# Cross-attention's planned order: the load queue chained into it, and key scaling planned no earlier than the block's start

## The chip, the cores and the metric

The kernel runs on one core of one Trainium2 chip. The metric is the time of one execution on the device in microseconds (us): the median over several runs, beside it the span and the instructions of one execution that was profiled.

## The reference

A two-layer encoder over 512 tokens of width 1024, all in float32. Each layer is a mixer, then memory cross-attention, then a gated convolutional FFN, each with a residual sum. Layer 0 mixes with forgetting and differential attention, layer 1 with a chunkwise mLSTM. The change lies in cross-attention (4 heads of 256, 256 memory tokens), which runs once per layer:

```python
def memory_cross_attention(xn, memn, wq, wkv, wo):
    q = split_heads(xn @ wq, XATTN_HEADS)
    k, v = jnp.split(memn @ wkv, 2, axis=-1)
    k = split_heads(k, XATTN_HEADS)
    v = split_heads(v, XATTN_HEADS)
    logits = jnp.einsum('bhqd,bhmd->bhqm', q, k, preferred_element_type=jnp.float32) * (XATTN_HEAD_DIM ** -0.5)
    p = jax.nn.softmax(logits, axis=-1)
    out = jnp.einsum('bhqm,bhmd->bhqd', p.astype(v.dtype), v)
    return merge_heads(out) @ wo
...
    for layer in range(DEPTH):
        ...
        x = x + mixed
        x = x + memory_cross_attention(rms_norm(x, xattn_norm[layer]), rms_norm(mem, mem_norm[layer]),
                                       xattn_wq[layer], xattn_wkv[layer], xattn_wo[layer])
```

## The kernel before, in words

**Products in three parts.** Every float32 operand is split into a high and a low part, and a product is three matmuls (high x high, high x low, low x high). The activations are held transposed, in eight tiles `x0` to `x7` of 128 x 512, with `xh`/`xl` beside them. A weight comes in chunks of 128 x 1024: SP loads it into one of three `raw` buffers, ScalarE (ACT) casts it to `wh`, and VectorE (DVE) subtracts to get `wl`, after which the raw buffer is free. `wh` and `wl` also have three buffers each, which the planner counts as `h` slots; such a slot is free when the chunk's matmuls are done.

**Cross-attention's stages on TensorE (PE).** (1) Two value blocks, the opening: V of 512 columns each, four chunks per block (c0 to c7 over both), two steps of six matmuls of 512 columns per chunk, into two accumulator banks per block (lines 1375 to 1377). In between come the eight small matmuls of the norm of x (line 1256). (2) The query projection: head 0 plainly (`plain`), heads 1 to 3 with seven instead of eight products of halves (`seven`), with the blocks of K and head 0's scores in between. (3) Scores, transposes, weighted values. (4) The output projection, eight blocks.

**What comes from the stage before.** The mixer's output projection is eight blocks of 5.2 us on PE; after each, DVE adds to `x` and the next stage's `xh`, `xl` and squares are made. Before it, two K products for the keys ("fills", each with two of the eight key blocks) were already made; they sit in two of the four accumulator banks until `keys` has scaled them. `keys(m)` multiplies the product by the memory's norm (DVE, into `kx`, one buffer), ACT casts it to `kt` and DVE subtracts the low part. The second `kx` of a pair frees the bank. The tiles of cross-attention's own pool (`kx`, `kt`, `sa`, `q` and others) lie in space which the mixer's pool held before; the pools for `raw`, `wh`, `wl` and `x` are shared by all stages.

**Other transfers of the stage.** `leave` stores each `x` tile to memory (`xs<-x`, line 1304), since the tiles are then used as room by the sevens; `back` loads it again before the output projection (`x<-xs`, line 1311). The planner lets `leave` follow `form`, which makes the sums of x that the sevens need. A seven loads one weight half into `sa` (two buffers), and POOL's queue adds another onto it by an accumulating transfer. All plain loads of this stage are issued at line 1193.

**What sets the order.** `Sched` is a planner that runs while the kernel is built. Each task has an engine, a duration, dependencies, a due time worked back from the matmul that needs it, and the buffers that it takes and frees; time 0 is the start of the opening on PE, and SP may begin 14 us and ACT and DVE 10.4 us ahead of it. It picks tasks engine by engine and calls each task's function, which emits the instructions. `after` is a lower limit on a task's planned time, and a buffer's slot holds the planned time from which it is free (line 1174 sets the three of `h`). The tile framework then schedules what was emitted on every engine by its own rules. For the engines in `ORDERED`, `planned(True)` ties each instruction to the one emitted before it on the same engine, so that the framework keeps the planner's order there. In the kernel before, these are DVE, ACT and POOL; PE and SP are not tied. The FFN's planner calls `planned` in the same way. On the chip each engine runs its instructions in order, and each waits for what its data need.

Of the kernel before, what the change touches and what calls it, by code (L numbers as in the profile page):

```python
# [62 lines left out]
def restored(ps):  # L63

    return ps.rearrange("p (k r) -> p r k", r=2)


def folded(ap):

    return ap.rearrange("p (r k) -> p r k", r=2)  # L70


ORDERED = ("vector", "scalar", "gpsimd")


class Item:
    def __init__(self, fn, dur, deps, prio, take, free, chain, pre, after, order, load, st):
        self.fn, self.dur, self.deps, self.prio, self.st = fn, dur, list(deps), prio, st
        self.take, self.free, self.chain, self.pre, self.after = take, free, chain, pre, after
        self.order, self.load = [o for o in order if o is not None], load  # L80
        self.ready = None
# [4 lines left out]
class Plan:  # L86
# [11 lines left out]
    def add(self, fn, dur=0.0, deps=(), prio=None, take=(), free=(), chain=(), pre=(), after=0.0, order=(), load=(), st=None, soon=False):  # L98
        it = Item(fn, dur, [d for d in deps if d is not None], len(self.items) if prio is None else prio, take, free, chain, pre, after, order, load, st)
        it.n, it.soon = len(self.items), soon  # L100
        self.items.append(it)
        return it
# [215 lines left out]
class Engines:  # L318
# [6 lines left out]
    def __getattr__(self, name):  # L325
        return getattr(self.nc, name)

    def planned(self, on):
        for c in self.chains:
            c.on, c.last = on, None  # L330


class Builder:
    def __init__(self, tc, t):
        self.tc, self.nc, self.t = tc, Engines(tc, ORDERED), t
        self.uid = 0
# [831 lines left out]
    def xattn_steps(self, layer, mp):  # L1168

        nc, t = self.nc, self.t  # L1170
        sc = Sched(
            WAIT, raw=3, h=3, sa=2, sb=2, ra=1, s2=1, a22=1, s4=1, qc=1, v=1, u2=1, u3=1, kx=1, q=6, kt=3, e=7, pt=2, acc=4, s=2, w=2
        )
        sc.slots.update(h=[-10.4, -5.2, 0.0])
        add = sc.add
        tt = lambda n: 0.055 + 1.06e-3 * n
        act = lambda n: 0.1 + 0.83e-3 * n
        tt_ = nc.vector.tensor_tensor
        clock = [0.0]
# [136 lines left out]
        def keys(m, get, deps, free=()):  # L1316
            st = {}

            def scaled():
                if m % 2 == 0:  # L1320
                    kt[m // 2] = self.til(mp, "kt", (P, 2, 2, MEM), F32R, bufs=3)
                st["x"] = self.til(mp, "kx", (P, MEM), bufs=1)
                tt_(out=folded(st["x"][:]), in0=restored(get()), in1=folded(self.memrb[:]), op=ALU.mult)

            take = [("kx", st)] + ([("kt", kst[m // 2])] if m % 2 == 0 else [])
            a = add("DVE", tt(256), scaled, deps, clock[0] + 0.5, take, free)
            h = add("ACT", act(256), lambda: nc.scalar.copy(kt[m // 2][:, 0, m % 2, :], st["x"][:]), [a], clock[0] + 1.0)
            kdone[m // 2].append(
                add("DVE", tt(256), lambda: self.sub(kt[m // 2][:, 1, m % 2, :], st["x"][:], kt[m // 2][:, 0, m % 2, :]), [h], clock[0] + 1.5, (), [("kx", st)])
            )  # L1330
# [3 lines left out]
        def key_block(m):  # L1334
            st, lo = weight(t["xk"][layer, m], clock[0])
            xh, xl = self.mems()
            last = None
            for c in range(2):

                def fn(c=c):  # L1340
                    if c == 0:
                        st["ps"] = self.acc_bank(st["_acc"])
                    for k in range(4 * c, 4 * c + 4):
                        s = slice(k * P, (k + 1) * P)
                        self.mm3(st["ps"][:, :MEM], st["wh"][:, s], st["wl"][:, s], xh[k], xl[k], k == 0, k == 7)

                last = pe(1.335, fn, [lo, last], [("acc", st)] if c == 0 else (), [("h", st)] if c else ())
                if c == 0:
                    yield
            keys(m, lambda: st["ps"][:, :MEM], [last], [("acc", st)])  # L1350
# [275 lines left out]
        for b, st in enumerate(self.fills):  # L1626
            st["_acc"] = st["banks"][0]
            sc.slots["acc"][st["_acc"]] = float("inf")
            sc.held.append(st)
            for i in range(2):  # L1630
                keys(2 * b + i, lambda st=st, i=i: st["ps"][:, i * MEM : i * MEM + MEM], (), [("acc", st)] if i else ())
# [19 lines left out]
        for k in range(4):  # L1651
            f, a, st = form(k, FORM + 4.0 * k)
# [36 lines left out]
        for m in range(8):  # L1689
            for _ in out_block(m):  # L1690
                pass
        nc.planned(True)
        sc.run()
        nc.planned(False)
        self.state = state


# [770 lines left out]
```

## Time and profile before

| | |
|---|---|
| median of 3 runs | 1422.31 us (1421.45 to 1422.38) |
| the profiled execution | 1424.06 us, of which the span is 1422.30 us |
| PE busy, matmuls | 1399.5 us, 98% of the span |
| DVE busy | 1169.5 us, 82% |
| ACT busy | 859.9 us, 60% |
| transfers | 204.75 MB, 144 GB/s in the mean |
| granted PE clock | 0.999 |
| openings of cross-attention | 254.45 to 281.96 us (layer 0), 940.61 to 968.12 us (layer 1) |

A time between two executions can differ by some tenths of a percent, and the span leaves out what lies around the first and last instruction. In rows of the profile, `L306` is the line through which nearly all instructions of DVE, ACT and POOL are emitted, so those are told apart by their tiles (`out<-in`); SP's rows are the issue of a transfer, not its duration.

### The profile page before, as it was taken

To read this page: it belongs to the slowest core of one execution; us is meant where nothing else is said; L and a number is where in the kernel's file an instruction comes from. 1 tells how busy PE (TensorE), PEld (TensorE's weight loads), DVE (VectorE), ACT (ScalarE), POOL (GpSimd) and SP (SyncE) were. 2 spreads that over 40 slices of the span, in tenths; PEclk is the share of its full clock that TensorE was granted. 3 is DMA by queue.
4 is the path that set the end of the run, shared out by engine and by line. 5 is a ranking of instruction groups with operands and counts; after the bars stand their busy time and mean duration, and the time that the engine had idled before them with its cause. 6 is when DMAs were issued, how large, how long until landed. Compare 5 with 4: busy or idle time off the path is not lost.

```text
span 1422.3 us, 22959 instructions
## 1 busy us (share of the span) xinstructions
PE 1399.5 (98%) x8660; PEld 1263.0 (89%) x8660; DVE 1169.5 (82%) x2006; ACT 859.9 (60%) x1444; POOL 138.4 (10%) x201
## 2 busy tenths in 40 slices
PE   9999999899999999999999999999999999999998
PEld 8888868799889999999888888979988999999997
DVE  7787786788689999999768876668877999999984
ACT  6797565666475656666456665456655665656655
POOL 0002220010001111110001121001000111111000
PEclk9999999999999999999999999999999999999999
DMA  5225325663258776774233332466413877777622
GB/s 205 90 58 152 111 81 180 212 161 116 90 156 222 185 182 175 188 178 118 73 116 103 128 98 80 159 190 185 149 60 122 212 198 176 191 177 187 142 75 80
DMA packets 77183, 204.75 MB, mean 144 GB/s; under 512 B 8352, under 2 KB 8352, under 8 KB 77072
## 3 DMA queue, kind: packets, MB, share of 16 engines
q1 hardware_dynamic: 61888, 163.44, 35.5%
q0 software_dynamic: 14176, 38.72, 15.8%
q8 instruction: 68, 1.11, 0.3%
q10 hardware_dynamic: 1008, 1.12, 0.2%
q14 instruction: 43, 0.35, 0.1%
HBM read 196.91 MB, written 6.34 MB: 143 GB/s over the span
## 4 chain that ended last, share of the span: by engine, by line
PE 83%; DVE 9%; ACT 3%; issue 2%; DMA 2%; POOL 0%; POOLq 0%; DVEq 0%; ACTq 0%
PE acc L384 17%; PE acc L385 17%; PE acc L386 17%; PE w L384 4%; PE w L386 4%; PE w L385 4%; PE s L384 3%; PE s L386 3%; PE s L385 3%; DVE wl L306 2%; PE acc L446 1%; PE acc L448 1%; PE acc L447 1%; DMA raw<-in_xv_dram 1%; PE w L2244 1%
## 5 line engine op out<-in xcount | busy, mean ns | idle before, releaser
L306 ACT CAST wh<-raw 128x1024 fp32r<-128x1024 f32 (+2 forms) x223 | 228.2, 1025 | 179.2 <-PE acc L385 90.5
L306 DVE TENSOR_TENSOR wl<-raw,wh 128x1024 fp32r<-128x1024 f32 (+2 forms) x223 | 267.0, 1198 | 40.0 <-ACT wh L306 39.3
L384 PE MATMUL acc<-xh,wh 128*128 128x512 f32 (+1 forms) x752 | 251.7, 335 | 0.0
L386 PE MATMUL acc<-xh,wl 128*128 128x512 f32 (+1 forms) x752 | 250.1, 333 | 0.0
L385 PE MATMUL acc<-xl,wh 128*128 128x512 f32 (+1 forms) x752 | 250.1, 333 | 0.0
L386 PEld LDWEIGHTS acc<-xh,wl 128*128 128x128 f32 x752 | 143.1, 190 | 11.1
L384 PEld LDWEIGHTS acc<-xh,wh 128*128 128x128 f32 x752 | 143.3, 191 | 10.2
L385 PEld LDWEIGHTS acc<-xl,wh 128*128 128x128 f32 x752 | 143.2, 190 | 10.2
L306 DVE SCALAR_TENSOR_TENSOR c<-hs,vec,c 128x512 f32<-128x512 f32 x176 | 131.8, 749 | 3.8 <-ACT c L306 0.8
L384 PE MATMUL w<-ah,wh 128*128 128x512 f32 x304 | 115.7, 381 | 0.2 <-ACT c L306 0.2
L385 PE MATMUL w<-al,wh 128*128 128x512 f32 x304 | 115.2, 379 | 0.0
L386 PE MATMUL w<-ah,wl 128*128 128x512 f32 x304 | 115.2, 379 | 0.0
L306 DVE TENSOR_TENSOR x<-acc,x 128x512 f32<-128x512 f32 (+1 forms) x43 | 28.0, 654 | 67.8 <-PE acc L386 67.8
L306 ACT CAST ah<-c 128x512 fp32r<-128x512 f32 x44 | 27.2, 619 | 85.5 <-DVE c L306 85.5
L306 ACT ACTIVATE c<-hs,vec 128x512 f32<-128x512 f32 x88 | 70.8, 812 | 13.1 <-DVE hs L306 8.8
L386 PEld LDWEIGHTS w<-ah,wl 128*128 128x128 f32 x304 | 57.5, 189 | 8.1
L384 PEld LDWEIGHTS w<-ah,wh 128*128 128x128 f32 x304 | 57.6, 190 | 7.9 <-DVE x L306 0.9
L385 PEld LDWEIGHTS w<-al,wh 128*128 128x128 f32 x304 | 57.6, 190 | 6.5
L386 PE MATMUL acc<-mem,wl 128*128 128x256 f32 (+1 forms) x192 | 59.6, 310 | 1.1 <-DVE wl L306 1.1
L384 PE MATMUL acc<-mem,wh 128*128 128x256 f32 (+1 forms) x192 | 59.6, 310 | 0.1
L385 PE MATMUL acc<-mem,wh 128*128 128x256 f32 (+1 forms) x192 | 59.5, 310 | 0.0
L306 POOL DMA_DIRECT2D sa<-in_up_dram x36 | 31.6, 877 | 279.0 <-DVE hs L306 114.3
(443 smaller groups left out, 4041.0 us busy)
## 6 DMA issues: line engine op xcount, KB each, us to landing
raw<-in_up_dram SPq DMA_DIRECT2D x52, 512.0 KB, 4.0
sa<-in_up_dram SPq DMA_DIRECT2D x36, 512.0 KB, 3.5
sa<-in_up_dram POOLq DMA_DIRECT2D x36, 512.0 KB, 6.7
raw<-in_down_dram SPq DMA_DIRECT2D x32, 512.0 KB, 4.1
ra<-in_up_dram SPq DMA_DIRECT2D x36, 256.0 KB, 4.4
sb<-in_up_dram POOLq DMA_DIRECT2D x36, 256.0 KB, 5.0
raw<-in_wo_dram SPq DMA_DIRECT2D x16, 512.0 KB, 4.0
raw<-in_xk_dram SPq DMA_DIRECT2D x16, 512.0 KB, 3.7
```

What stands on the lines that cost most here:

```text
L306: i = issue(*a, **k)
L384: mm(out, wh, xh, start=first, stop=False, skip_group_check=parts)
L385: mm(out, wh, xl, start=False, stop=False, skip_group_check=parts)
L386: mm(out, wl, xh, start=False, stop=last, skip_group_check=parts)
L446: mm(ps, xh[k][:, ts], wh, start=(k == 0), stop=False)
L447: mm(ps, xh[k][:, ts], wl, start=False, stop=False)
L448: mm(ps, xl[k][:, ts], wh, start=False, stop=(k == 7))
L2244: nc.tensor.matmul(ps[:, lo:], vv[s][:, c], a[:], start=(s == 0), stop=(s == 3))
```

## The change

Three edits, all in how cross-attention is planned:

- SP is wrapped like the other ordered engines, and cross-attention ties all four in the planner's order. `planned` takes how many engines it ties, three unless told otherwise, so the FFN's order is tied as before.
- The slots of `sa` are free in the plan from 1.0 on, instead of from -14.
- The first operation of `keys`, the multiplication into `kx`, is planned at 0.3 at the earliest. Without a limit it could be planned from -10.4 on, when DVE's plan begins.

No instruction is added or removed.

```diff
-ORDERED = ("vector", "scalar", "gpsimd")
+ORDERED = ("vector", "scalar", "gpsimd", "sync")
...
-    def planned(self, on):
-        for c in self.chains:
+    def planned(self, on, n=3):
+        for c in self.chains[:n]:
             c.on, c.last = on, None
...
-        sc.slots.update(h=[-10.4, -5.2, 0.0])
+        sc.slots.update(h=[-10.4, -5.2, 0.0], sa=[1.0, 1.0])
...
-            a = add("DVE", tt(256), scaled, deps, clock[0] + 0.5, take, free)
+            a = add("DVE", tt(256), scaled, deps, clock[0] + 0.5, take, free, after=0.3)
...
-        nc.planned(True)
+        nc.planned(True, 4)
         sc.run()
-        nc.planned(False)
+        nc.planned(False, 4)
```

## The prediction

> **What bounds the kernel now.** I read the busy shares first, then the matmul engine's waits over the whole span, then a table of windows, and last the timelines of PE, DVE, ACT and SP around one of those waits. Busy time and waits come first:
>
> ```profile
> PE 1399.5 (98%) x8660; PEld 1263.0 (89%) x8660; DVE 1169.5 (82%) x2006; ACT 859.9 (60%) x1444; POOL 138.4 (10%) x201
> PE acc L1376 <- DVE wl L306: 5.5, 8, 1.0
> PE acc L1375 <- ACT wh L306: 1.6, 2, 1.0
> ```
>
> PE is busy for 1399.5 of 1422.3 us, so only its gaps can be won. The two longest rows of its waits (us in total, times, longest) belong to L1375 and L1376, matmuls of the value blocks with which cross-attention opens. The windows of layer 0's opening and of the stretch behind it show it (columns: window, length, busy us of PE, its loads, DVE, ACT, POOL, granted clock, DMA share, GB/s):
>
> ```profile
> 254.40:282.00 27.60, 23.31 (x106) 18.77 (x106) 22.76 (x36) 19.81 (x28) 1.78 (x2) 1.00 0.79 237
> 282.00:300.00 18.00, 18.00 (x118) 16.71 (x117) 16.58 (x25) 10.93 (x17) 5.13 (x4) 1.00 0.69 188
> ```
>
> PE is full behind the opening and has holes inside it. Now the PE timeline there (start, duration, tile, and in brackets the idle time before it with what ended it):
>
> ```profile
> 254.45 0.38 PE L1375 MATMUL acc<-wh,mem 128*128 128x512 f32 x1
> 255.40 0.48 PE L1375 MATMUL acc<-wh,mem 128*128 128x512 f32 x1 [0.57 <-DVE x L306]
> 256.86 0.48 PE L1376 MATMUL acc<-wl,mem 128*128 128x512 f32 x1 [0.98 <-DVE wl L306]
> 259.56 0.95 PE L1256 MATMUL s<-ones,sq 128*128 128x2 f32 x8
> 260.37 0.46 PE L1376 MATMUL acc<-wl,mem 128*128 128x512 f32 x1
> 263.82 0.38 PE L1377 MATMUL acc<-wh,mem 128*128 128x512 f32 x1
> ...
> 268.13 0.38 PE L1377 MATMUL acc<-wh,mem 128*128 128x512 f32 x1
> 269.55 0.48 PE L1375 MATMUL acc<-wh,mem 128*128 128x512 f32 x1 [1.04 <-ACT wh L306]
> 270.81 0.48 PE L1376 MATMUL acc<-wl,mem 128*128 128x512 f32 x1 [0.78 <-DVE wl L306]
> 279.48 0.48 PE L1376 MATMUL acc<-wl,mem 128*128 128x512 f32 x1 [0.64 <-DVE wl L306]
> 281.96 0.38 PE L384 MATMUL acc<-xh,wh 128*128 128x512 f32 x1
> ...
> 940.61 0.38 PE L1375 MATMUL acc<-wh,mem 128*128 128x512 f32 x1
> 968.12 0.38 PE L384 MATMUL acc<-xh,wh 128*128 128x512 f32 x1
> ```
>
> The pace of full matmuls is 0.216 us (20 of them from 263.82 to 268.13). The opening holds 16 steps of 6 such matmuls, 96 x 0.216 = 20.7 us, and the eight small ones of L1256, 0.8 us (259.56 to 260.37): 21.5 us. It lasts from 254.45 to 281.96, and in layer 1 from 940.61 to 968.12: 27.5 us each. So each opening loses 6.0 us, 11.9 us both together before rounding, more than the brackets add up to since a matmul after a wait is also 0.1 us slower.
>
> **Why it waits.** The eight chunks of the value weights (c0 to c7) go through three raw buffers: load (SP), `wh` (ACT), `wl` (DVE), which frees the buffer. Here are these engines:
>
> ```profile
> 244.12 1.05 ACT L306 CAST wh<-raw 128x1024 fp32r<-128x1024 f32 x1 [2.99 <-issue]
> 249.47 0.69 DVE L306 TENSOR_TENSOR x<-acc,x 128x512 f32<-128x512 f32 x1 [2.29 <-PE acc L386]
> 252.06 1.46 SPq L1193 DMA_DIRECT2D sa<-in_xq_dram  x2
> 254.65 0.69 DVE L306 TENSOR_TENSOR x<-acc,x 128x512 f32<-128x512 f32 x1 [2.34 <-PE acc L386]
> 255.26 0.41 DVE L306 TENSOR_TENSOR kx<-acc,memrb 128x256 f32<-128x256 f32 x1
> 255.59 1.22 DVE L306 TENSOR_TENSOR wl<-raw,wh 128x1024 fp32r<-128x1024 f32 x1
> 256.53 0.39 ACT L306 CAST kt<-kx 128x256 fp32r<-128x256 f32 x1
> 256.82 1.04 ACT L306 CAST wh<-raw 128x1024 fp32r<-128x1024 f32 x1
> 256.87 0.34 SPq L1193 DMA_DIRECT2D raw<-in_xv_dram  x1
> 258.78 1.22 DVE L306 TENSOR_TENSOR wl<-raw,wh 128x1024 fp32r<-128x1024 f32 x1
> 260.03 8.33 DMA raw<-in_xv_dram
> 265.37 0.42 DVE L306 TENSOR_TENSOR kx<-acc,memrb 128x256 f32<-128x256 f32 x1
> 272.01 1.22 DVE L306 TENSOR_TENSOR wl<-raw,wh 128x1024 fp32r<-128x1024 f32 x1
> 285.28 0.69 DVE L306 TENSOR_TENSOR x<-sa,raw 128x512 f32<-128x512 f32 x1
> ```
>
> c0's `wh` is done at 245.2, yet its `wl` runs at 255.59, though DVE stood idle for over 2 us twice in between. What stands ahead of it on DVE is the key scaling `kx`, at 255.26, directly behind the last `x` of the output projection. The plan allows `kx` at once and DVE is held to the plan's order, but on the chip `kx` comes only with the end of the projection. I infer that its space belongs to the stage before until then; the trace doesn't name that wait. ACT does the same one step on: c1's `wh` (256.82) stands behind `kt` (256.53). So the buffers are freed late: c3's load goes at 256.87, when c0's `wl` ends, c4's at 260.03, when c1's ends, and c4's load, 8.33 us on the chain of waits, makes the holes at 269.55 and 270.81.
>
> **The change, part by part.**
>
> *Keys not before 0.3.* `kx` and all behind it on its chain leave the front of the order; no instruction is added. c0's `wl` can then follow its `wh`, at about 245.2. c1's `wh` needs an h slot, free when the projection's seventh block ends (its `x` is at 249.47), so its `wl` is at about 250.4 to 251.6, in idle time of DVE. It pushes that block's later vector work by about 1 us; no matmul waits for that. c3's load then goes at 246.4 and c4's at 251.7, 10.5 and 8.3 us sooner. From there, with t = 0 at 254.45 and chunks of 12 x 0.216 = 2.59 us:
>
> - First matmuls: c0 is ready; the second accumulator bank still waits for `x` (254.65 + 0.69), so the wait that 255.40 ends is the next limit. 0.65 us of matmuls fit before it: 0.3 us, 0.4 with the slow matmul. This remains.
> - c3 and c4 are in memory before their h slots are free: nothing.
> - c2, c3 and c4 get their h slots at the ends of the projection, of c0 and of c1: t = 0, 3.0 and 6.4 (with the hole above and 0.8 of small matmuls). 1.05 of ACT and 1.22 of DVE later their raw buffers are free, and the loads of c5, c6 and c7 go at about 2.5, 5.4 and 8.7. With the slow 8.33 us landing and again ACT and DVE they are ready at 13.1, 16.0 and 19.3; PE wants them at 14.2, 16.8 and 19.4, so they just fit. The first query weight behind them (load at 13.1) would be ready at 23.7 against 22.0: 1.7 us late, or, with the median landing of 4.7 us (below), early. I take 0.5.
> - DVE: 22.76 us busy of 27.60 now; two `wl` leave it (2.4), so 20.3 stand against 22.8. It is nearly full, and the last hole (279.48, 0.64 idle, 0.8 with the slow start) was its lateness. I keep half, 0.4.
>
> *The load queue in the plan's order, `sa` from 1.0.* This moves two kinds of transfers past others on SP:
>
> ```profile
> raw<-in_xv_dram SPq DMA_DIRECT2D x8, 512.0 KB, 4.7
> xs<-x SPq DMA_DIRECT2D x5, 256.0 KB, 2.0
> 216.19 0.92 SPq L1304 DMA_DIRECT2D xs<-x  x2
> 257.26 0.42 SPq L1304 DMA_DIRECT2D xs<-x  x1
> 286.00 0.62 ACT L306 CAST x<-x 128x512 fp32r<-128x512 f32 x1 [1.06 <-DVE x L306]
> 356.37 13.54 SPq L1193 DMA_DIRECT2D raw<-in_xo_dram  x3
> 364.88 0.69 DVE L306 TENSOR_TENSOR x<-acc,x 128x512 f32<-128x512 f32 x1 [2.57 <-PE acc L386]
> ```
>
> The eight stores of x (`xs`, 216 to 257) now go as each block is done. The plan puts them behind the forms, so they fall into the opening and shortly after; each lands in 2.0 us, and the first cast that overwrites such an x is at 286.00. One wait is new on SP: a seven's half weight goes into the room of an `x` tile and must wait for that tile's store, which now stands shortly ahead of it; for up to those 2.0 us the query weights behind it wait too, which the 0.5 above may take in. `sa` goes behind c3's and c4's loads instead of at 252.06; it is used at 285.28. The reloads of x are planned later than they run now; their first use is at 364.88, so even from behind the load at 356.37 the first, half the size of a weight's, would land in time at the 4.7 us of a weight. POOL's accumulates onto `sa` move with it, by a few us and with 20 to spare. I put this part at zero; its bounds are the rivals below: a gain it can't give beyond the 11.9, the loss in the first rival.
>
> *Sum.* 6.0 - (0.4 + 0.5 + 0.4) = 4.7 us an opening, 9.3 us for two, since PE is full behind them. The profiled execution took 1424.06 us (span 1422.30, 1.76 around it), so it would be 1414.8. The median of three is 1422.31, 1.75 below the profiled one; from it 1413.0.
>
> **Rivals.**
>
> *The transfers bound the opening.* It moves 237 GB/s x 27.6 = 6.5 MB at a DMA share of 0.79, 21.8 us of transfer. Seven stores of x come in (1.8 MB), c3 and c4 go out (1.0 MB): 7.3 MB, 24.4 us at the same rate. If all of it lies in the opening, 3.1 us are won in each: 1416.1. For it: the 8.33 us landing. Against: the stores are behind the urgent loads in the plan, and nothing needs them before 286. The Trainium skill ("DMA: Bandwidth & Descriptors", Issuing engines are not separate DMA queues) says that transfers issued by SP and POOL share the same 16 engines and interleave. By that rule the stores and POOL's accumulates slow the value loads wherever they meet, which is this rival; the slow landing agrees. The skill's "Perfetto Trace Analysis" (Optimization Strategy) reads a repeated gap as too few buffers for the next tile. By it the three raw buffers would hold PE whatever the order, and the last rival would come out; the trace speaks against it, since c0's `wl`, which frees one, waited 10 us on an idle DVE.
>
> *Slower: the keys hold the banks.* The keys' results sit in two accumulator banks until `kx` of the second and fourth has run, and the second value block takes these two. PE comes to it at 254.45 + 0.4 + 48 x 0.216 + 0.8 = 266.0. Today the fourth `kx` is at 265.37, without harm, as PE is there only at 269.55. If the new plan lets it fall behind the `wl` of 272.01, it ends at 273.7 and PE waits 7.7 us: 7.7 + 0.9 - 6.0 = 2.6 lost per layer, 1427.5. It decides from about 270.7 on. Against it: the plan computes due times back from the matmul that takes the bank, and the queue of `wl` is shorter by two.
>
> *It does nothing.* If c0's `wl` waits for something else than `kx` (its own buffer, say), the holes stay: 1422. Against it: c0's `wh` was written at 244.12, so its slot was free.
>
> **How the numbers follow.** The forecast has 0.57, with its own range from 1410.4 (no hole left) to 1415. Transfers 0.22 (1415 to 1418), no effect 0.13, banks 0.06, and 0.02 for a loss I don't see, slower too. Faster is then 0.79, within 0.2% (2.8 us, about what can be told here) 0.13, slower 0.08. The range from 1410.4 to 1418.0 holds 0.79.
>
> **What would show it.** Right: `wl` on DVE near 245 and 250 ahead of the first `kx`, loads of the value weights near 246 and 252, the opening at 22 to 23.5 us, no 1 us hole at its fifth chunk, stores of x behind 262. Wrong: `wl` still behind `kx`; PE waiting for `kx` near 266; SP idle in front of a store or `sa` with value loads behind it; new holes after 282.

## The result, and the profile after

The changed kernel takes 1411.57 us (median of four runs, 1410.82 to 1412.64) against 1422.28 us, a ratio of 0.9927 (95% interval 0.9909 to 0.9944): 10.7 us faster. The prediction said 1413.0 us, with a range of 1410.4 to 1418.0. The profiled execution took 1412.64 us, its span 1410.9 us.

The same views as before, first the busy shares and the top row of PE's waits over the whole span:

```profile
PE 1397.0 (99%) x8660; PEld 1263.2 (90%) x8660; DVE 1170.0 (83%) x2006; ACT 859.7 (61%) x1444; POOL 135.4 (10%) x201
PE s L794 <- DVE sm L306: 1.1, 3, 0.4
```

The rows of L1375 and L1376, which stood at the top, are gone from that list. Next the windows of the two openings and of the stretch behind the first (window, length, busy us of PE, its loads, DVE, ACT, POOL, granted clock, DMA share, GB/s), and PE's timeline at their edges:

```profile
253.30:275.40 22.10, 22.09 (x106) 18.83 (x104) 18.95 (x29) 17.45 (x25) 1.78 (x2) 1.00 0.90 274
275.40:293.40 18.00, 18.00 (x118) 16.71 (x117) 17.76 (x28) 12.32 (x18) 0.85 (x1) 1.00 0.80 248
934.20:956.40 22.20, 22.19 (x107) 18.92 (x106) 20.19 (x32) 18.77 (x26) 1.80 (x2) 1.00 0.91 271
```

```profile
253.32 0.38 PE L1375 MATMUL acc<-wh,mem 128*128 128x512 f32 x1
...
253.97 0.78 PE L1375 MATMUL acc<-wh,mem 128*128 128x512 f32 x2
254.59 0.38 PE L1376 MATMUL acc<-wl,mem 128*128 128x512 f32 x1
...
265.19 0.38 PE L1377 MATMUL acc<-wh,mem 128*128 128x512 f32 x1
265.58 0.48 PE L1375 MATMUL acc<-wh,mem 128*128 128x512 f32 x1
...
275.40 0.38 PE L384 MATMUL acc<-xh,wh 128*128 128x512 f32 x1
...
934.28 0.38 PE L1375 MATMUL acc<-wh,mem 128*128 128x512 f32 x1
...
956.36 0.38 PE L384 MATMUL acc<-xh,wh 128*128 128x512 f32 x1
```

Each opening now lasts 22.08 us (253.32 to 275.40, 934.28 to 956.36) instead of 27.51: 5.43 us less in each, 10.9 us together, which is the whole difference of the medians. What is left over the 21.5 us of matmuls is 0.2 us at the second bank (the second of the two matmuls at 253.97 waits, so that the next comes at 254.59) and 0.3 us at the second value block (265.58, a late start and a slow matmul). The spans of the two profiled executions differ by a little more, 11.4 us: the first opening already begins 1.1 us earlier, and the rest of the program is 0.6 us slower. In the eleven kernels of this record that opening begins anywhere from 252.21 to 254.45 us, so I put neither difference down to the change. Now DVE, ACT and SP at the first opening:

```profile
242.99 1.05 ACT L306 CAST wh<-raw 128x1024 fp32r<-128x1024 f32 x1 [2.99 <-issue]
244.07 1.23 DVE L306 TENSOR_TENSOR wl<-raw,wh 128x1024 fp32r<-128x1024 f32 x1 [0.21 <-ACT wh L306]
245.32 0.33 SPq L306 DMA_DIRECT2D raw<-in_xv_dram  x1
248.12 1.06 ACT L306 CAST wh<-raw 128x1024 fp32r<-128x1024 f32 x1 [2.94 <-PE acc L385]
249.21 1.23 DVE L306 TENSOR_TENSOR wl<-raw,wh 128x1024 fp32r<-128x1024 f32 x1 [0.18 <-ACT wh L306]
250.47 0.33 SPq L306 DMA_DIRECT2D raw<-in_xv_dram  x1
255.52 0.42 DVE L306 TENSOR_TENSOR kx<-acc,memrb 128x256 f32<-128x256 f32 x1
...
262.54 0.43 SPq L306 DMA_DIRECT2D xs<-x  x1
265.10 0.43 DVE L306 TENSOR_TENSOR kx<-acc,memrb 128x256 f32<-128x256 f32 x1
282.70 2.33 SPq L306 DMA_DIRECT2D xs<-x  x4
```

Both early `wl` follow their `wh` within 0.2 us, ahead of the first `kx`. The loads of c3 and c4 go as each ends, at 8.0 and 2.8 us ahead of the opening's start; before, c4's went 5.6 us behind it. The stores of x lie in the opening and behind it, four of them from 282.70 on.

The 0.3 us at the second value block are a wait for `kx`. The matmul before it starts at 265.19, so at 0.216 us each PE would go on at 265.41; the fourth `kx`, which frees the bank, ends at 265.53, and PE goes on at 265.58. The weights were not late: the `wl` of that chunk (c4) was done at 262.1. The list of waits in the opening (waiting engine and line, what it waited for; us in total, times, longest) names `kx` as what PE's weight load waited for, with the same row in layer 1:

```profile
PEld acc L1375 <- DVE kx L306: 0.4, 1, 0.4
```

### The profile page after: what moved, and what is told of

Read it like the earlier page. It is cut to its first block, busy times and chain, and to the rows that moved or that the text cites. A ratio compares the mean times of both kernels' runs of the same rounds, so it can differ in the third digit from the quotient of the medians.

```text
span 1410.9 us, 22975 instructions
## 1 busy us (share of the span) xinstructions
PE 1397.0 (99%) x8660; PEld 1263.2 (90%) x8660; DVE 1170.0 (83%) x2006; ACT 859.7 (61%) x1444; POOL 135.4 (10%) x201
## 4 chain that ended last, share of the span: by engine, by line
PE 86%; DVE 7%; issue 3%; ACT 3%; DMA 1%; POOL 1%; POOLq 0%; DVEq 0%; ACTq 0%
PE acc L384 17%; PE acc L385 17%; PE acc L386 17%; PE w L384 4%; PE w L386 4%; PE w L385 4%; PE s L384 3%; PE s L386 3%; PE s L385 3%; PE acc L446 1%; PE acc L448 1%; PE acc L447 1%; PE w L2244 1%; PE acc L1375 1%; DVE wl L306 1%
## 5 line engine op out<-in xcount | busy, mean ns | idle before, releaser
L306 DVE TENSOR_TENSOR x<-acc,x 128x512 f32<-128x512 f32 (+1 forms) x43 | 28.0, 653 | 65.7 <-PE acc L386 65.7
```

The lines of the kernel that those rows point to most:

```text
L306: i = issue(*a, **k)
```

## Experiments

The theory: the key scaling at the front of DVE's and ACT's planned order held back the first two value chunks and so the loads behind them, and that alone cost the time. Main rival: the loads' own order on SP.

**The key limit alone** (the kernel before with `after=0.3`; SP not tied, `sa` as before):

```diff
-            a = add("DVE", tt(256), scaled, deps, clock[0] + 0.5, take, free)
+            a = add("DVE", tt(256), scaled, deps, clock[0] + 0.5, take, free, after=0.3)
```

> The kernel before with the limit of 0.3 on kx alone; SP is not tied and sa's slots are as before. Theory (the keys at the front of DVE's order are the whole cause): both openings 22 to 23 us, total 1411 to 1413 us, and the stores of x still go at the end of each projection block. Rival (the load order in the plan brings the gain): openings near 27.5 us, 1421 to 1423 us. Between them: 1414 to 1419 us, and the openings say how it is shared.

Measured 1411.69 us, ratio 0.9923 (0.9910 to 0.9935), openings of 22.55 and 22.28 us. The key limit is the whole gain; the rival falls. On SP, not tied:

```profile
244.78 0.33 SPq L1193 DMA_DIRECT2D raw<-in_xv_dram  x1
248.52 0.33 SPq L1304 DMA_DIRECT2D xs<-x  x1
249.93 0.33 SPq L1193 DMA_DIRECT2D raw<-in_xv_dram  x1
250.39 1.45 SPq L1193 DMA_DIRECT2D sa<-in_xq_dram  x2
```

The stores go early as before, yet c3's and c4's loads move just the same: they had waited for a buffer, not for their turn.

**The load queue and `sa` alone** (the changed kernel without the key limit):

```diff
-            a = add("DVE", tt(256), scaled, deps, clock[0] + 0.5, take, free, after=0.3)
+            a = add("DVE", tt(256), scaled, deps, clock[0] + 0.5, take, free)
```

> The changed kernel with kx unlimited again: SP tied, sa from 1.0. Theory: c0's wl still waits behind kx until about 255, openings 26.5 to 28 us, total 1421 to 1423 us. Rival (the load order): openings 22 to 24 us, 1411 to 1414 us. If the stores that are now issued inside the opening cost anything, it shows here as more than 1423 us.

Measured 1423.39 us, ratio 1.0004 (0.9995 to 1.0013): no change, and what lies above the expected 1423 is within the noise. The openings are 29.38 us, above the expected 26.5 to 28, and 26.50 us. In the first, the chain of waits, then PE's timeline and its windows:

```profile
266.49 9.68 DMA raw<-in_xv_dram
277.37 0.48 PE L1375 MATMUL acc<-wh,mem 128*128 128x512 f32 x1 [2.46 <-ACT wh L306]
278.63 0.48 PE L1376 MATMUL acc<-wl,mem 128*128 128x512 f32 x1 [0.78 <-DVE wl L306]
...
272.00:278.60 6.60, 3.39 (x15) 2.23 (x13) 2.12 (x4) 2.28 (x3) 0.00 (x0) 1.00 1.05 328
278.60:283.40 4.80, 4.77 (x14) 3.92 (x15) 4.80 (x10) 2.43 (x3) 0.00 (x0) 0.64 0.87 320
```

In this stretch PE does wait for transfers: with the value loads still late and the stores moved among them, the DMA share is 1.05 and a value chunk takes 9.68 us to land; another 1.3 us of this opening are a slow clock (last section). That is the prediction's first rival, at work in a kernel whose loads have no lead. It shows in one opening of two: in layer 1, where the stores are moved as well, no hole is longer than 1 us, and the opening is 1.0 us shorter than in the kernel before, with 1.1 us of waits right behind it.

**The changed kernel without the `sa` edit** (`sa` free in the plan from -14, SP tied):

```diff
-        sc.slots.update(h=[-10.4, -5.2, 0.0], sa=[1.0, 1.0])
+        sc.slots.update(h=[-10.4, -5.2, 0.0])
```

> The changed kernel with sa's slots free in the plan from -14 again; SP tied, keys limited. Theory: sa is planned ahead of c3's load, its room is free only 2 to 3 us ahead of the opening, so SP holds c3's load back from 8 us to 2 or 3 us ahead of the opening and c4's a little; both have that slack, so 1411 to 1413 us. Rival (the sa slots are what makes the tied queue safe): c3 and c4 come late, holes at the fourth and fifth chunk of 1 to 3 us in each opening, 1413 to 1418 us.

Measured 1413.10 us, ratio 0.9933 (0.9920 to 0.9945), where the two expectations meet; the interval overlaps that of the changed kernel. Openings of 24.13 and 21.94 us. In the first:

```profile
250.74 1.45 SPq L306 DMA_DIRECT2D sa<-in_xq_dram  x2
252.29 13.39 SPq L306 DMA_DIRECT2D raw<-in_xv_dram  x5
267.06 0.48 PE L1375 MATMUL acc<-wh,mem 128*128 128x512 f32 x1 [0.33 <-ACT wh L306]
```

c3's load stands behind both `sa` loads until 252.29, 0.9 us ahead of the opening instead of 8.0. It lands in 7.6 us and c4's in 9.2, and the slack doesn't quite cover that: 2 us are lost, in holes at the fifth and sixth chunk. In layer 1 c3's load goes later still, with the start of the opening (935.92 against 935.90), but lands in 5.0 us, and nothing is lost; two accumulates are issued in the first of these openings, one in the second. So the lead that the tied queue takes away costs time only where the loads also land slowly. The rival is right in one layer of one execution: the `sa` edit belongs to the tied queue, and what it is worth isn't clear of the noise.

**Keys and `sa`, SP not tied** (the kernel before with these two edits):

```diff
-        sc.slots.update(h=[-10.4, -5.2, 0.0])
+        sc.slots.update(h=[-10.4, -5.2, 0.0], sa=[1.0, 1.0])
...
-            a = add("DVE", tt(256), scaled, deps, clock[0] + 0.5, take, free)
+            a = add("DVE", tt(256), scaled, deps, clock[0] + 0.5, take, free, after=0.3)
```

> Keys limited and sa from 1.0, SP not tied. Theory: as with the keys alone, 1411 to 1413 us, since the framework's own order on SP was not what made the holes. Rival: without the tie the new plan's loads come in a worse order, 1414 to 1419 us.

Measured 1411.49 us, ratio 0.9922 (0.9908 to 0.9935), openings of 22.35 and 22.08 us: the same as the changed kernel. Tying SP brings nothing that can be measured.

**The keys late** (the changed kernel with the limit at 12):

```diff
-            a = add("DVE", tt(256), scaled, deps, clock[0] + 0.5, take, free, after=0.3)
+            a = add("DVE", tt(256), scaled, deps, clock[0] + 0.5, take, free, after=12.0)
```

> The changed kernel with the limit on kx at 12.0 instead of 0.3. Theory with the banks (the rival of the prediction as a mechanism): the second value block reaches PE about 12 us after the opening's start and then waits for the fourth kx, which ends at about 17 to 19 us: a hole of 4 to 7 us in each opening, openings of 26 to 29 us, total 1420 to 1426 us. If the banks don't hold PE, the openings stay near 22 us and the total at 1411 to 1414 us.

Measured 1417.13 us, ratio 0.9957 (0.9942 to 0.9972): 5.6 us slower than the changed kernel, between the two expectations. Openings of 25.75 and 24.21 us, each with one hole, shown here in PE's timeline of both layers and the windows around them:

```profile
266.26 0.74 PE L1375 MATMUL acc<-wh,mem 128*128 128x512 f32 x1 [2.00 <-DVE xvl L306]
950.87 0.48 PE L1375 MATMUL acc<-wh,mem 128*128 128x512 f32 x1 [2.00 <-DVE xvl L306]
263.90:269.80 5.90, 3.90 (x11) 2.82 (x10) 5.55 (x10) 4.50 (x8) 0.00 (x0) 0.71 1.05 324
948.50:953.00 4.50, 2.50 (x12) 1.81 (x10) 4.19 (x7) 4.10 (x7) 0.00 (x0) 1.00 1.06 319
```

The second value block waits for `xvl`, the results of the first block, not for `kx`: the planner takes the banks that are free first in its plan, and with late keys those are the first block's own. Keys that come too late make a hole of 2 us in each opening, not of 4 to 7; in layer 0 a slow clock behind it adds 1.5 us (clock 0.71 in the first window).

**`kx` in other room, the plan as before** (`rb` is the norm's tile in a pool of its own, free at that time):

```diff
-            ("kt", (P, 2, 2, MEM), F32R, 3), ("kx", (P, MEM), F32, 1),
+            ("kt", (P, 2, 2, MEM), F32R, 3),
...
-                st["x"] = self.til(mp, "kx", (P, MEM), bufs=1)
+                st["x"] = self.til(self.sp, "rb", bufs=1)[:, :MEM]
```

> The kernel before, with kx placed in the room of the norm's rb tile, which is free at that time, instead of cross-attention's own pool. Theory (kx waits for space of the mixer's pool): the first kx runs during the output projection and c0's wl near 245 us, so the hole for c0's wl (1.2 us) goes and c3's load moves to about 246; kt is still in the pool, so c1's wh and wl stay behind it and c4's load stays near 257 to 259: openings of 25 to 27 us, total 1417 to 1421 us. Rival (kx waits for something else, its input or DVE's own order): nothing moves, openings 27.5, 1421 to 1423 us.

Measured 1416.72 us, ratio 0.9956 (0.9939 to 0.9973), openings of 24.91 and 25.03 us, just under what was expected. The timelines of DVE and ACT (`rb` is now `kx`):

```profile
223.93 0.42 DVE L306 TENSOR_TENSOR rb<-acc,memrb 128x256 f32<-128x256 f32 x1
242.96 1.23 DVE L306 TENSOR_TENSOR wl<-raw,wh 128x1024 fp32r<-128x1024 f32 x1 [0.22 <-ACT wh L306]
249.11 0.39 ACT L306 CAST kt<-rb 128x256 fp32r<-128x256 f32 x1
253.02 0.41 DVE L306 TENSOR_TENSOR kt<-rb,kt 128x256 fp32r<-128x256 f32 x1
253.47 0.42 DVE L306 TENSOR_TENSOR rb<-acc,memrb 128x256 f32<-128x256 f32 x1
253.81 1.22 DVE L306 TENSOR_TENSOR wl<-raw,wh 128x1024 fp32r<-128x1024 f32 x1
```

With nothing changed but its place, the first `kx` runs at 223.93, 28 us ahead of the opening, and no longer holds c0's `wl`, which runs at 242.96. So it was the space that `kx` waited for. `kt`, still in the pool, is written only at 249.11, and c1's `wl` stands behind its low part and the second `kx` until 253.81. Why that low part waits on from 249.5 to 253.02, the trace doesn't name.

**`kx` between the first two chunks** (the changed kernel with the limit at -6):

```diff
-            a = add("DVE", tt(256), scaled, deps, clock[0] + 0.5, take, free, after=0.3)
+            a = add("DVE", tt(256), scaled, deps, clock[0] + 0.5, take, free, after=-6.0)
```

> The changed kernel with the limit on kx at -6.0, so that the plan has c0's wl ahead of the first kx and c1's wl behind it. Theory (each wl that stands behind kx delays the load two or three chunks on): c0's hole is gone, c4's load stays at 257 to 260 and the holes at the fifth chunk stay or grow; openings 24 to 27.5 us, total 1416 to 1422 us. Rival (only the first wl matters): openings 22 to 23 us, 1411 to 1413 us.

Measured 1419.93 us, ratio 0.9980 (0.9971 to 0.9989), openings of 25.71 and 24.47 us, inside the expected ranges, though not by the expected holes. The hole for c0 is gone, and c1's `wl` is behind `kx` (DVE's and PE's timelines):

```profile
243.67 1.22 DVE L306 TENSOR_TENSOR wl<-raw,wh 128x1024 fp32r<-128x1024 f32 x1 [0.21 <-ACT wh L306]
253.73 0.41 DVE L306 TENSOR_TENSOR kx<-acc,memrb 128x256 f32<-128x256 f32 x1
254.06 1.21 DVE L306 TENSOR_TENSOR wl<-raw,wh 128x1024 fp32r<-128x1024 f32 x1
271.19 0.70 PE L1375 MATMUL acc<-wh,mem 128*128 128x512 f32 x2 [0.96 <-ACT wh L306]
```

c4's load goes at 255.34, 2.4 us behind the start of the opening (5.6 in the kernel before), and lands in 3.4 us, so the hole at the fifth chunk is gone too. The holes come at the seventh chunk (the row at 271.19) and in layer 0 at the eighth. That a `wl` behind `kx` costs time holds; that it shows two or three chunks on does not.

**`sa` later in the plan, SP not tied** (the kernel before):

```diff
-        sc.slots.update(h=[-10.4, -5.2, 0.0])
+        sc.slots.update(h=[-10.4, -5.2, 0.0], sa=[9.0, 9.0])
```

> The kernel before with sa's slots free in the plan from 9.0 on; SP not tied, keys unlimited. It takes the loads of sa and POOL's accumulates away from c4's load. Theory (the 8.3 us landing of c4 is contention with them): c4 lands in 4 to 6 us, its holes of 2.2 us shrink by 1.5 to 2.2 us in each opening, total 1418 to 1420 us. Rival (the landing is slow for another reason, or the holes come from ACT and DVE): holes as before, 1421 to 1423 us.

Measured 1422.73 us, ratio 0.9997 (0.9987 to 1.0006), openings of 28.19 and 27.59 us; c4's load lands in 8.2 us. It doesn't settle what makes the landing slow: with SP not tied the framework issued both `sa` loads from 250.25 on, 2.4 us ahead of the opening as before, and the accumulates with them. The next run takes the accumulates away.

**Without the accumulates** (the kernel before; the second weight half is not added onto `sa`):

```diff
-            b1 = onto(lambda: sa["sa"][:], lambda: A2, 1024, [b1], at - 16.0)
```

> The kernel before without POOL's accumulating transfers onto sa in cross-attention (three a layer), so the second weight half is not added. Nothing else of the order is touched. Theory (c4's 8.3 us landing is contention with the accumulates): c4 lands in 4 to 5 us, the two holes at the fifth chunk (2.2 us) go or fall under 0.5, the holes at c0 and c1 stay, openings of 25 to 26 us, total 1417 to 1420 us. Rival (the landing is slow by the number of plain loads in flight): c4 lands in 7 us or more and the openings stay above 27 us.

Measured 1416.81 us, ratio 0.9961 (0.9947 to 0.9975); both openings 24.68 us, 2.8 us shorter; all three are a little better than expected. PE's longest hole and its last one, then the load of c4 and how long it took to land, min, median and max of that one load:

```profile
255.52 0.48 PE L1376 MATMUL acc<-wl,mem 128*128 128x512 f32 x1 [0.98 <-DVE wl L306]
275.31 0.48 PE L1376 MATMUL acc<-wl,mem 128*128 128x512 f32 x1 [0.16 <-DVE wl L306]
...
258.69 0.33 SPq L1193 DMA_DIRECT2D raw<-in_xv_dram  x1
DMA to landing us min/median/max: 3.2/3.2/3.2
```

The landing falls from 8.3 us to 3.2 us, the holes at the fifth chunk are gone, the last hole falls from 0.64 to 0.16 us, and those ahead of the fifth chunk stay. So of the 6.0 us that an opening lost, about 2.8 were the accumulates, met by loads that came late. The changed kernel keeps the accumulates and still gains 5.4 us an opening, since its loads have their lead.

## Why the prediction was right, point by point

- **The cause.** That `kx` stands ahead of c0's `wl` and waits for the space of the stage before was inferred; the run with `kx` in other room shows it. The key limit alone gives the whole gain.
- **The early loads.** Forecast for c0's `wl` 9.2 us ahead of the opening, for the loads of c3 and c4 8.0 and 2.8 us; measured 9.2, 8.0 and 2.8. The loads of c5, c6 and c7 were forecast at about 2.5, 5.4 and 8.7 us behind its start; measured 2.3, 5.3 and 8.9.
- **The sum.** Forecast 4.7 us an opening, measured 5.43. The mis-sized terms are the three that should remain: the bank 0.4 (it is 0.2: PE fits four matmuls of the first chunk ahead of the wait, not three), late landings 0.5 (0.0: c5, c6 and c7 land in 3.7, 7.7 and 5.4 us, ACT waits 0.5 us for one of them and PE for none, and PE is full behind the opening), DVE's lateness 0.4 (0.0, though DVE is busy for 18.95 of 22.10 us). One that the sum left out came in: 0.3 us for the fourth `kx`.
- **The holes of the kernel before.** The prediction gives the slow matmul after a wait as the reason why an opening loses more than its brackets add up to. In layer 0 the brackets add up to 4.3 us, and six slow matmuls make 0.6 of the 1.7 that are missing. Most of the rest is that a bracket counts from the end of a matmul's row, 0.38 us after its start, while the next could start after 0.216: 0.16 a hole, 1.0 us in all.
- **The stores.** They were priced at nothing, and cost nothing that the runs with and without the tied queue can tell, but they landed far slower than the 2.0 us used. That was the median of stores issued ahead of the opening; the one that the kernel before issued inside its opening (257.26) took 8.5 us. These are the landings of transfers issued inside the changed opening (count, KB, median us):

```profile
raw<-in_xv_dram SPq DMA_DIRECT2D x3, 512.0 KB, 5.4
xs<-x SPq DMA_DIRECT2D x4, 256.0 KB, 5.8
```

- **Rival: the transfers bound the opening.** Not in the changed kernel, but near: the DMA share rose from 0.79 to 0.90, on 6.06 MB (274 GB/s x 22.1 us) instead of the 7.3 MB of that sum, mostly since half of the stores fall behind the opening. In the kernel with the queue alone they do, in one opening of two. The rule of the Trainium skill ("DMA: Bandwidth & Descriptors", Issuing engines are not separate DMA queues), that SP's and POOL's transfers share the same engines, is what the run without accumulates agrees with: 8.3 to 3.2 us. The other page that the prediction names, the Trainium skill's "Perfetto Trace Analysis" (Optimization Strategy), says of a repeated gap that it can mean too few buffers for the next tile. Here it was one of order: the same three buffers are enough in the changed kernel.
- **Rival: the keys hold the banks.** Its mechanism is there, and small: in the changed kernel the second block does take a bank of the keys and waits for the fourth `kx` near 266, for 0.3 us instead of 7.7. Its step from late keys to a large loss fell: the plan takes whichever banks are free first. The late-keys run, with a limit 12 us on, loses 3.7 and 2.1 us an opening against the changed kernel and is still faster than the kernel before.
- **Rival: it does nothing.** Excluded by the run with the key limit alone.

## What to carry to other kernels

When an engine is held to a planned order, one operation that the plan allows earlier than its space allows is a plug: everything behind it waits, on an engine that looks idle. Look for a wait whose own input was long ready, and ask what stands ahead of it in program order and what that one waits for; giving the plan the true earliest time of a single operation was worth 10.7 us here. If a load queue is tied to the same order too, every load on it needs its true earliest time as well, or the plug moves there: behind the `sa` loads it cost 2 us in one opening.

## What the runs showed of the hardware

After some short waits of PE its granted clock fell, and after others as long it did not. In the first opening of the queue-alone kernel, after holes of 2.46 and 0.78 us, eight matmuls (six in the opening, two behind it) ran at 0.43 us instead of 0.216, with a granted clock of 0.64 in that window: 1.7 us on top. With late keys the same 2.00 us hole did so in layer 0 (clock 0.71) and not in layer 1 (1.00), and the kernel with `sa` late in the plan lost clock after holes of 0.93 and 0.78 us, while the kernel before passed 1.04 and 0.78 at 1.00; this is its window behind them:

```profile
269.30:273.30 4.00, 4.00 (x13) 3.20 (x12) 4.00 (x7) 4.00 (x6) 0.00 (x0) 0.57 0.60 199
```

The Trainium skill ("TensorE: Matmul & The Clock Gate", What's actually happening) puts the slow state, at half the clock, behind an idle window of about 3.4 us that runs freely. The halved pace agrees; the single holes were shorter, 2.46 us and less. What decides between two equal holes was not measured.

The accumulating transfers were dear. In the changed opening POOL's queue moved 1.05 MB for 24.1% of the DMA engines' time and SP's 5.00 MB for 65.7%, 1.7 times as much per byte. POOL's queue carried only accumulates there, so what of this is the accumulation and what the queue isn't told apart:

```profile
q1 hardware_dynamic: 1851, 5.00, 65.7%
q0 software_dynamic: 288, 1.05, 24.1%
```
